# Hybrid encoder block: the output projection takes its PSUM banks one at a time, in another chunk order, and the order planner waits longer before transposes

## The chip, the cores and the metric

The kernel runs on one core of one Trainium2 chip. The metric is the device time of one execution, in microseconds (us). The profiled execution also has a span, from its first to its last instruction; about 2.2 us of the device time lie outside it.

## The reference, cut to what matters

The input is x, 1024 tokens of 1024 channels, float32. One layer, then a last RMSNorm:

```python
hn = rms_norm(h, ln_g)
proj = hn @ w_in + b_in                      # 1024 x 3584
glu_a, glu_b, z_conv, q, k, v, z_att = split(proj)   # 512 columns each
y_conv = conformer_conv(glu_a, glu_b, ...)   # GLU, depthwise conv of 31 taps, LayerNorm, swish, 512 x 512 product
y_att  = neighbourhood_attention(q, k, v, rpb)       # 8 heads of 64 on a 16 x 64 grid, window 8 x 16
y_conv = grouped_rms_norm(y_conv, ..., 8) * silu(z_conv)
y_att  = grouped_rms_norm(y_att, ..., 8) * silu(z_att)
h = h + concatenate([y_conv, y_att]) @ w_out         # 1024 x 1024
out = rms_norm(h, final_g)
```

## The kernel before, in words

Every float32 product is made of three matmuls: each operand is split into a high part in a rounded float32 format (ACT copies it) and a low part, the rest (DVE or POOL subtracts), and high x high, low x high and high x low are added up in one PSUM bank. PSUM has eight banks of 128x512 float32; the program names them by tags: two each of `pj`, `s` and `tr`, one each of `o` and `ln`.

**The order planner.** The instructions of PE, ACT, DVE, POOL and SP stay in the order in which the program emits them, and each engine works through its own queue in that order. The order comes out of a planner, `Clock` (from line 93). The work is written as some dozens of Python generators ("streams") with a rank. The planner has a time of its own, `now`, which a matmul moves on by its planned duration (`mm`, `tp`), and a planned end for each of ACT, DVE and POOL (`queue`). A stream that yields a time is not taken up before `now` has come to it; among the streams that are due, `weave` (line 113) takes the one of lowest rank. Nothing waits on the chip for a planned time: what is planned sets only the order in each queue. On the chip, semaphores hold an instruction back until its inputs and its buffer are there, and all that is behind it on its engine with it. `Ring` (line 74) hands out buffers and banks by the same planned time.

**Margins.** A stream that wants to put a matmul or a transpose on PE after work on another engine yields the planned end of this work plus a margin. `PEL` (0.3) stands at the four places of `pointwise` (lines 864, 887, 907 and 928), `PEA` (0.15) in `stats` (312), in `turns` (739, the transposes of the softmax), in `attention` (782 before the products with v, for each of two groups of a block, and 794 before the transposes of the result), and in `head_out` (817, before the transposes of a pair of heads).

**The stages.** After the normalisation come the input projections (`proj`), the convolution's taps on DVE (`taps`) and the attention, 32 blocks of scores, softmax, turns and products with v. Then `pointwise(t)`, once for each of eight tiles of 128 tokens: transposes into bank `tr` (tile ln), LayerNorm, transposes into bank `ln` (lnb), the 512 x 512 product in bank `ln` (pw), the grouped norm, and transposes back into bank `ln` (yt). A tile holds one of two buffers (xn) from its start to its yt, so that tile t+2 starts when tile t is through. The end of yt on ACT is noted in `ln_end[t]`.

**The last gates.** `final_gates` (from line 1074) makes the last two column blocks of z_conv for both halves of the tokens: four banks, `pj`, `pj`, `s`, `s`, 96 matmuls into tiles pz. `gated` (from line 953) then works off each bank: tanh on ACT into tile gz, two DVE instructions into z, which frees the bank, and a product on DVE that puts z into acc, the convolution's half of y. There is one gz buffer, so the four follow one another.

**The output projection.** The 1024 rows of w_out are eight chunks k of 128. Chunks 0 to 3 are of the convolution, 4 to 7 of the attention; `K_OUT` is 4, 5, 6, 7, 0, 1, 2, 3. `out_weights` splits the chunks into woh and wol (the low parts by turns on POOL and DVE). `split_y` splits y for each tile of tokens into yh and yl, from ya (attention) and acc (convolution); a tile 3 to 7 does so when buffers come free. `out_mm` (line 1152) emits the three matmuls of a tile, a chunk and a piece of columns (two pieces of 512 per tile; the last tile has 512, 256, 256). `finish` adds x, squares and sums on ACT, scales, and sends the tile out. `out_proj` (from line 1197) sets the order. It begins when all eight `ln_end` are there. Tiles 0, 1 and 2 go together: it first takes six banks (tr, tr, o, ln, pj, pj), and then goes chunk by chunk through all six. Tiles 3 to 7 come one by one, each piece with all its eight chunks. x_again loads x again for `finish`, two tiles ahead.

Of the kernel before, what the change touches and what calls it, by code (L numbers as in the profile page):

```python
# [21 lines left out]
NT = T // P  # L22
# [29 lines left out]
PQ = 0.2  # L52
KHY = (0, 1, 2)
BV = ("o", "ln")
PEL, PEA, PEB, MMO = 0.3, 0.15, 0.15, 0.0137
W_AHEAD = 12
TQ = 0.4
TURN = 0.02
# [8 lines left out]
def size(ap):  # L67
    n = 1
    for d in ap.shape[1:]:
        n *= d  # L70
    return n
# [88 lines left out]
def block(ctx: ExitStack, tc: tile.TileContext, x, xt, vecs, w_in, taps_w, pw_w, pw_b, tab0, tab1, tab2, w_out, final_g, out):  # L160
# [14 lines left out]
    ck = Clock(nc)  # L175
# [5 lines left out]
    RB, NB = {"pj": r_pj, "s": r_s, "tr": r_tr, "o": r_o, "ln": r_ln}, {"pj": 2, "s": 2, "tr": 2, "o": 1, "ln": 1}  # L181
    r_hn, r_hy = ring(0), ring(0)

    def U(name, dt=F32, shape=(P, 1024)):
        return big.tile(list(shape), dt, tag="u", name=name)

    def half_tile(tag, name, dt=F32, bufs=1):
        return att.tile([P, 512], dt, tag=tag, bufs=bufs, name=name)
# [4 lines left out]
    def bank(tag, name, bufs=2):  # L193
        return ps.tile([P, 512], F32, tag=tag, bufs=bufs, name=name)
# [460 lines left out]
    def group_scale(src, ms, sq, sums=None):  # L655

        g = sq.rearrange("p (g d) -> p g d", d=64)
        t = ck.act(out=g, in_=src, func=AF.Square, scale=0.125)
        yield t
        t = ck.dve("tensor_reduce", t, in_=g, out=ms, axis=mybir.AxisListType.X, op=ALU.add) + 0.5  # L660
        ck.q["dve"] = t
        if sums is None:
            t = ck.dve("tensor_scalar", out=ms, in0=ms, scalar1=EPS, scalar2=None, op0=ALU.add)
        else:
            ck.dve("scalar_tensor_tensor", out=sums, in0=sums, scalar=EPS, in1=sums, op0=ALU.mult, op1=ALU.mult)
            t = ck.dve("tensor_tensor", out=ms, in0=ms, in1=sums, op=ALU.add)
        yield t
        t = ck.gps("tensor_tensor", 1.65, t, out=ms, in0=ms, in1=mhalf, op=ALU.pow)
        return t


    def grid(ap):
        return ap.rearrange("p (r c) -> p r c", c=GW)
# [93 lines left out]
    def attention():  # L767
        for n, (i, a, b) in enumerate(blocks):
# [34 lines left out]
            if b < 3:  # L803
                r_o.put(t)
            else:
                ck.spawn(head_out(i, a, ytok, po), -1)

    def head_out(i, a, ytok, po):
        ms = sm.tile([P, 8], F32, tag="ms", name=f"ams{2 * i + a}")
        src = ytok[:, :, a, :]  # L810
        t = yield from group_scale(src, ms, po, sumss[2 * i + a])
        r_o.put(t - 1.6)
        t = ck.gps("tensor_tensor", 1.05, t, out=src, in0=src, in1=ms.unsqueeze(2).broadcast_to([P, 8, 64]), op=ALU.mult)
        if a == 0:
            return
        yield from r_u.get()
        yield t + PEA
        y = U(f"ya{i}")
        yg = grid(y)
        for b2 in range(2):  # L820
            yield from r_tr.get()
            pt = bank("tr", f"yat{i}_{b2}")
            for e in range(4):
                ck.tp(pt[:, e * P:(e + 1) * P], ytok[:, 4 * b2 + e].rearrange("p a d -> p (a d)"), ident)
            for b in range(2):
                c0 = 32 * b2 + 16 * b
                t = ck.act(out=yg[:, :, c0:c0 + 16],
                           in_=pt[:, 256 * b:256 * b + 256].rearrange("p (r c) -> p r c", c=16),
                           func=AF.Copy, scale=hcol(V_GNA + i))
            r_tr.put(t)  # L830
            yield
        r_y.put()
        ya[i] = y, t
# [208 lines left out]
    K_OUT = list(range(4, 8)) + list(range(4))  # L1042
# [109 lines left out]
    def out_mm(po, t, k, sl):  # L1152
        while (t, k) not in ysp or k not in woh:
            yield ck.now + 0.1
        yh, yl, a = ysp[t, k]
        yield max(a, woh[k][1])
        ck.mm(po, yh[:, k, :], woh[k][0][:, sl], k == K_OUT[0], False)
        ck.mm(po, yh[:, k, :], wol[k][:, sl], False, False)
        ck.mm(po, yl[:, k, :], woh[k][0][:, sl], False, k == K_OUT[-1])

    def pieces(t):

        ends = (0, 512, 768, 1024) if t == NT - 1 else (0, 512, 1024)
        return [slice(a, b) for a, b in zip(ends, ends[1:])]

    def finish(t, n, sl, po, ss):
        while t not in xr:
            yield ck.now + 0.1
        x_ = xr[t][:, sl]
        e = ck.dve("tensor_tensor", out=x_, in0=po, in1=x_, op=ALU.add)  # L1170
        yield e
        junk = half_tile(("uh", "ul")[n % 2], f"oj{t}_{n}", bufs=1 + n % 2)[:, :size(po)]
        e = ck.act(e, out=junk, in_=x_, func=AF.Square, scale=1.0 / 32.0, accum_out=ss[:, n:n + 1])
        ck.dve("tensor_tensor", out=x_, in0=x_, in1=fg[:, sl], op=ALU.mult)
        yield e
        if n == 0:
            ck.gps("tensor_scalar", 0.2, e, out=ss[:, 0:1], in0=ss[:, 0:1], scalar1=EPS, scalar2=None, op0=ALU.add)
            return
        e = ck.gps("tensor_tensor", 0.3, e, out=ss[:, 0:1], in0=ss[:, 0:1], in1=ss[:, n:n + 1], op=ALU.add)
        if sl.stop < D:  # L1180
            return
        rs = sm.tile([P, 1], F32, tag="rs", name=f"ors{t}")
        e = ck.gps("tensor_tensor", 0.47, e, out=rs, in0=ss[:, 0:1], in1=mhalf[:, :1], op=ALU.pow)
        yield e
        for m in range(2):
            x_ = xr[t][:, 512 * m:512 * m + 512]
            if m == 0:
                d = ck.dve("tensor_scalar", e, 0.55, out=x_, in0=x_, scalar1=rs, scalar2=None, op0=ALU.mult)
            else:
                d = ck.act(e, out=x_, in_=x_, func=AF.Copy, scale=rs)  # L1190
            yield d
            nc.sync.dma_start(out=out2[t * P:(t + 1) * P, 512 * m:512 * m + 512], in_=x_)
        r_u.put(d + 3.0)
        r_xr.put(d + 3.0)
        state["out"] = t

    def out_proj():
        tags = ("tr", "tr", "o", "ln", "pj", "pj", "s", "s")
        i = 0
        while len(ln_end) < NT:  # L1200
            yield ck.now + 0.2
        for ts in ((0, 1, 2), (3,), (4,), (5,), (6,), (7,)):
            po, ss = {}, {}
            for t in ts:
                ss[t] = sm.tile([P, 3], F32, tag="st", name=f"oss{t}")
                for n, sl in enumerate(pieces(t)):
                    tag = tags[i % 8]
                    i += 1
                    yield from RB[tag].get()
                    po[t, n] = bank(tag, f"out{t}_{n}", NB[tag])[:, :sl.stop - sl.start], tag  # L1210
            if len(ts) > 1:
                for k in K_OUT:
                    for t in ts:
                        for n, sl in enumerate(pieces(t)):
                            yield from out_mm(po[t, n][0], t, k, sl)
                for t in ts:
                    for n, sl in enumerate(pieces(t)):
                        ck.spawn(finish(t, n, sl, po[t, n][0], ss[t]), -1)
                        RB[po[t, n][1]].put(ck.now + 1.5)
            else:  # L1220
                t = ts[0]
                for n, sl in enumerate(pieces(t)):
                    for k in K_OUT:
                        yield from out_mm(po[t, n][0], t, k, sl)
                    ck.spawn(finish(t, n, sl, po[t, n][0], ss[t]), -1)
                    RB[po[t, n][1]].put(ck.now + 1.0)
                    yield
            for t in ts:
                for _ in range(2):
                    (r_hy if t % 4 < 3 else r_u).put()  # L1230

    fgs = []

# [14 lines left out]
    ck.spawn(out_tiles(), 0)  # L1248
    ck.spawn(x_again(), 0)
    ck.spawn(out_proj(), 6)  # L1250
    ck.weave(lambda: state["out"] == NT - 1 and len(ck.streams) == 0)
    in_order.__exit__(None, None, None)
# [47 lines left out]
```

## Time and profile before

| what | us |
|---|---|
| median of 3 runs | 570.06 (568.01 to 571.66) |
| the profiled execution | 567.91 |
| its span | 565.7 |
| PE busy | 529.6 (94%) |
| DVE busy | 430.3 (76%) |
| ACT busy | 274.1 (48%) |
| POOL busy | 172.0 (30%) |

The page gives busy time by engine, the span in 40 slices, the chain of work that ended last and the costliest groups. PE is TensorE, PEld its weight loads, DVE is VectorE, ACT is ScalarE, POOL is GpSimd, SP issues the DMAs. Matmuls overlap, and the ends of their rows are modelled: what counts is the distance from one start to the next. L130 and L136 are the helper lines of matmul and transpose, L141, L145 and L150 those of ACT, DVE and POOL, so that a row is told apart by its tiles (out<-woh,yh).

### The profile page before, as it was taken

How to read it: one execution, taken by the hardware profiler on the slowest of the kernel's cores; microseconds unless marked ns; L12 is line 12 of the kernel's file. 1: busy time of each engine (PE TensorE's matmuls, PEld its weight loads, DVE VectorE, ACT ScalarE, POOL GpSimd, SP SyncE). 2: the span in 40 equal slices, each digit the busy share in tenths (PEclk: the TensorE clock that was granted, in tenths of full speed). 3: DMA queues.
4: the chain of work that ended last, by engine and by line, in shares of the span. 5: the costliest groups of instructions: out<-in, count | busy, mean ns of one | idle time of the engine just before them, and what ended most of it. 6: DMA issues, size and time to landing. Idle time of an engine off the chain costs nothing. (4 is left out here: it accounts for less than half of the span.)

```text
span 565.7 us, 7506 instructions
## 1 busy us (share of the span) xinstructions
PE 529.6 (94%) x2656; PEld 438.2 (77%) x2656; DVE 430.3 (76%) x709; ACT 274.1 (48%) x656; POOL 172.0 (30%) x142
## 2 busy tenths in 40 slices
PE   5998999999999999989998999998999977999995
PEld 4886788898878888878876787786877765888884
DVE  4459999989999989999899988767645468056342
ACT  7765421265633555535563755848455462053221
POOL 4422232221043404060043545226254270022121
PEclk9999999999999999999999999999999996999999
DMA  8941115521225331453234341010006311004442
GB/s 303 405 154 49 37 37 147 133 85 42 84 64 143 94 96 46 105 130 103 76 95 121 77 132 64 22 38 5 34 0 261 112 35 41 0 1 148 162 136 75
DMA packets 22613, 55.04 MB, mean 97 GB/s; under 512 B 3120, under 2 KB 3248, under 8 KB 22576
## 3 DMA queue, kind: packets, MB, share of 16 engines
q1 hardware_dynamic: 22288, 54.47, 30.8%
q8 instruction: 21, 0.34, 0.3%
q14 instruction: 16, 0.13, 0.1%
q10 hardware_dynamic: 288, 0.09, 0.1%
HBM read 40.92 MB, written 4.19 MB: 80 GB/s over the span
## 5 line engine op out<-in xcount | busy, mean ns | idle before, releaser
L145 DVE SCALAR_TENSOR_TENSOR acc<-glu,dwc,acc 128x512 f32<-128x512 f32 (+25 forms) x150 | 172.9, 1182 | 0.7
L150 POOL TENSOR_TENSOR wl<-wr,wh 128x512 fp32r<-128x512 f32 x48 | 79.7, 1677 | 200.0 <-ACT wh L141 200.0
L130 PE MATMUL out<-woh,yh 128*128 128x512 f32 (+1 forms) x136 | 53.0, 390 | 7.1 <-DVE z L145 7.1
L130 PE MATMUL pz<-hi,wh 128*128 128x512 f32 x128 | 53.2, 415 | 1.1 <-DVE ya L145 1.1
L130 PE MATMUL out<-wol,yh 128*128 128x512 f32 (+1 forms) x136 | 52.5, 386 | 0.0
L130 PE MATMUL out<-woh,yl 128*128 128x512 f32 (+1 forms) x136 | 52.5, 386 | 0.0
L130 PE MATMUL pz<-hi,wl 128*128 128x512 f32 x128 | 50.2, 392 | 0.0
L130 PE MATMUL pz<-lo,wh 128*128 128x512 f32 x128 | 50.1, 392 | 0.0
L141 ACT ACTIVATE prob<-s,mx 128x264 f32<-128x264 f32 (+1 forms) x64 | 33.4, 528 | 27.2 <-DVE mx L145 27.1
L141 ACT ACTIVATE wh<-wr 128x512 fp32r<-128x512 f32 x56 | 32.5, 625 | 23.0 <-DMA wr<-in_w_in 7.7
L145 DVE TENSOR_TENSOR xr<-out,xr 128x512 f32<-128x512 f32 (+1 forms) x17 | 11.0, 658 | 39.8 <-PE out L130 31.0
L145 DVE TENSOR_TENSOR ptl<-ptp,pth 128x512 fp32r<-128x512 f32 x64 | 37.8, 614 | 0.0
L141 ACT ACTIVATE pth<-ptp 128x512 fp32r<-128x512 f32 x64 | 32.5, 547 | 9.5 <-PE ptp L136 8.4
L130 PEld LDWEIGHTS out<-woh,yh 128*128 128x128 f32 x136 | 26.4, 194 | 13.1 <-DVE z L145 8.3
L136 PE MATMUL ptp<-ident,prob 128*128 128x128 f32 x224 | 32.8, 273 | 1.5 <-DVE ptl L145 1.4
L130 PE MATMUL pb<-hi,wh 128*128 128x512 f32 x64 | 26.2, 410 | 7.4 <-ACT wh L141 5.5
L145 DVE CUSTOM_DVE_ANT_0 s<-s,bias 128x264 f32<-128x264 f32 (+1 forms) x64 | 30.2, 511 | 0.9 <-PE s L130 0.9
L130 PE MATMUL po<-pth,v 128*128 128x256 f32 x112 | 29.8, 291 | 0.6 <-DVE v L145 0.4
L130 PE MATMUL po<-ptl,v 128*128 128x256 f32 x112 | 29.3, 290 | 1.1 <-DVE ptl L145 1.1
L130 PEld LDWEIGHTS out<-wol,yh 128*128 128x128 f32 x136 | 26.5, 195 | 4.9
L130 PEld LDWEIGHTS out<-woh,yl 128*128 128x128 f32 x136 | 26.3, 194 | 5.0
L136 PEld LDWEIGHTS ptp<-ident,prob 128*128 128x128 f32 x224 | 25.9, 140 | 4.7 <-issue 2.0
(151 smaller groups left out, 1352.6 us busy)
## 6 DMA issues: line engine op xcount, KB each, us to landing
wr<-in_w_in SPq DMA_DIRECT2D x27, 512.0 KB, 3.7
bias<-in_tab SPq DMA_DIRECT2D x16, 276.0 KB, 2.8
xc<-in_xt SPq DMA_DIRECT2D x16, 256.0 KB, 5.4
acc<-in_x SPq DMA_DIRECT2D x8, 512.0 KB, 6.3
wor<-in_w_out SPq DMA_DIRECT2D x8, 512.0 KB, 5.0
xr<-in_x SPq DMA_DIRECT2D x8, 512.0 KB, 3.8
out<-xr SPq DMA_DIRECT2D x16, 256.0 KB, 2.3
kh<-kh SPq DMA_DIRECT2D x24, 128.0 KB, 2.4
```

The lines of the kernel that those rows point to most:

```text
L130: self.nc.tensor.matmul(out, lhsT=lhsT, rhs=rhs, start=start, stop=stop)
L136: self.nc.tensor.transpose(out=out, in_=in_, identity=identity)
L141: self.nc.scalar.activation(**k)
L145: getattr(self.nc.vector, fn)(**k)
L150: getattr(self.nc.gpsimd, fn)(**k)
```

## The change

Two constants become larger, one margin in `head_out` changes its name, and the loops of `out_proj` are written anew. A function `part(t, ks)` emits the matmuls of tile t and chunks ks, piece by piece, and takes a bank only when it comes to a piece that has none. It is called for tiles 0, 1, 2 with the four chunks of the attention, then for tiles 0, 1, 2 with the four of the convolution, then for tiles 3 to 7 with all eight. `finish` is started after a piece's last chunk. The order in which the tags are used and the start condition on `ln_end` stay.

```diff
-PEL, PEA, PEB, MMO = 0.3, 0.15, 0.15, 0.0137
+PEL, PEA, PEB, MMO = 0.8, 0.3, 0.15, 0.0137
...
@@ head_out
         yield from r_u.get()
-        yield t + PEA
+        yield t + PEL
         y = U(f"ya{i}")
...
@@ out_proj
-        for ts in ((0, 1, 2), (3,), (4,), (5,), (6,), (7,)):
-            po, ss = {}, {}
-            for t in ts:
+        po, ss = {}, {}
+
+        def part(t, ks):
+
+            if t not in ss:
                 ss[t] = sm.tile([P, 3], F32, tag="st", name=f"oss{t}")
-                for n, sl in enumerate(pieces(t)):
-                    tag = tags[i % 8]
-                    i += 1
-                    yield from RB[tag].get()
-                    po[t, n] = bank(tag, f"out{t}_{n}", NB[tag])[:, :sl.stop - sl.start], tag
-            if len(ts) > 1:
-                for k in K_OUT:
-                    for t in ts:
-                        for n, sl in enumerate(pieces(t)):
-                            yield from out_mm(po[t, n][0], t, k, sl)
-                for t in ts:
-                    for n, sl in enumerate(pieces(t)):
-                        ck.spawn(finish(t, n, sl, po[t, n][0], ss[t]), -1)
-                        RB[po[t, n][1]].put(ck.now + 1.5)
-            else:
-                t = ts[0]
-                for n, sl in enumerate(pieces(t)):
-                    for k in K_OUT:
-                        yield from out_mm(po[t, n][0], t, k, sl)
+            for n, sl in enumerate(pieces(t)):
+                if (t, n) not in po:
+                    yield from banks(t, n, sl)
+                for k in ks:
+                    yield from out_mm(po[t, n][0], t, k, sl)
+                if ks[-1] == K_OUT[-1]:
                     ck.spawn(finish(t, n, sl, po[t, n][0], ss[t]), -1)
                     RB[po[t, n][1]].put(ck.now + 1.0)
                     yield
-            for t in ts:
+            if ks[-1] == K_OUT[-1]:
                 for _ in range(2):
                     (r_hy if t % 4 < 3 else r_u).put()
+
+        def banks(t, n, sl):
+            nonlocal i
+            tag = tags[i % 8]
+            i += 1
+            yield from RB[tag].get()
+            po[t, n] = bank(tag, f"out{t}_{n}", NB[tag])[:, :sl.stop - sl.start], tag
+
+        for t in range(3):
+            yield from part(t, K_OUT[:4])
+        for t in range(3):
+            yield from part(t, K_OUT[4:])
+        for t in range(3, NT):
+            yield from part(t, K_OUT)
```

## Rows read from the trace of the kernel before

**Rows 1.** The windows: PE, PEld, DVE, ACT, POOL busy, granted clock, DMA share, GB/s.
```profile
50.00:350.00 300.00, 288.94 (x1512) 241.34 (x1510) 286.83 (x442) 142.23 (x349) 88.72 (x52) 1.00 0.33 92
```

**Rows 2.** The chain that ended last, in order of time: start, us, what.
```profile
456.61 3.92 PE pz L130 x17
...
472.22 86.93 PE out L130 x393
...
561.38 0.72 ACT xr L141
```

**Rows 3.** Waits of PE over the span: us in total, times, longest.
```profile
PE out L130 <- DVE z L145: 7.1, 2, 6.2
...
PE lnb L136 <- DVE xn L145: 3.3, 3, 1.1
...
PE yat L136 <- POOL ytok L150: 1.8, 2, 1.5
...
PE yt L136 <- POOL xn L150: 1.1, 2, 0.8
PE po L130 <- DVE ptl L145: 1.1, 5, 0.3
```

**Rows 4.** Windows of tile out: us, PE busy, PEld busy, DVE busy, granted clock, DMA.
```profile
460.58:463.50 2.92, 2.88 (x12) 2.07 (x11) 0.00 (x0) 1.00 0.01 3
463.50:469.63 6.13, 0.00 (x0) 0.00 (x1) 0.00 (x0) 0.84 0.24 86
469.63:477.51 7.88, 6.94 (x16) 4.98 (x16) 0.00 (x0) 0.50 0.21 67
477.51:500.51 23.00, 23.00 (x102) 19.03 (x101) 0.00 (x0) 0.99 0.00 1
500.51:552.00 51.49, 51.49 (x229) 42.66 (x228) 9.44 (x14) 1.00 0.36 123
```

**Rows 5.** Timeline of all engines between the last gates and the output projection.
```profile
449.01 0.42 DVE L145 TENSOR_TENSOR yl<-acc,yh 128x256 fp32r<-128x256 f32 x1
...
454.33 0.28 DVE L145 TENSOR_TENSOR yl<-ya,yh 128x128 fp32r<-128x128 f32 x1
...
459.23 1.21 DVE L145 TENSOR_TENSOR wol<-wor,woh 128x1024 fp32r<-128x1024 f32 x1
...
460.58 0.39 PE L130 MATMUL out<-woh,yh 128*128 128x512 f32 x1
...
462.65 5.80 DVE L145 TENSOR_TENSOR wol<-wor,woh 128x1024 fp32r<-128x1024 f32 x2 [2.21 <-issue]
...
468.82 0.75 DVE L145 SCALAR_TENSOR_TENSOR z<-pz,cols,gz 128x512 f32<-128x512 f32 x1
...
469.63 0.79 PE L130 MATMUL out<-woh,yh 128*128 128x512 f32 x1 [6.17 <-DVE z L145]
...
471.42 0.75 DVE L145 SCALAR_TENSOR_TENSOR z<-pz,cols,gz 128x512 f32<-128x512 f32 x1
...
472.22 0.80 PE L130 MATMUL out<-woh,yh 128*128 128x512 f32 x1 [0.94 <-DVE z L145]
...
477.09 1.43 DVE L145 TENSOR_TENSOR yl<-acc,yh 128x256 fp32r<-128x256 f32 x4
```

**Rows 6.** Timeline of PE: the transposes that end pointwise tiles 1, 3, 5 and 7.
```profile
351.87 0.66 PE L136 MATMUL yt<-ident,xn 128*128 128x128 f32 x4 [0.84 <-POOL xn L150]
...
385.20 0.60 PE L136 MATMUL yt<-ident,xn 128*128 128x128 f32 x4
...
425.55 0.60 PE L136 MATMUL yt<-ident,xn 128*128 128x128 f32 x4
...
456.01 0.60 PE L136 MATMUL yt<-ident,xn 128*128 128x128 f32 x4
```

**Rows 7.** Timeline of SP: the loads of x for the finish, two by two.
```profile
464.11 9.13 SPq L1150 DMA_DIRECT2D xr<-in_x  x2
...
512.73 2.34 SPq L1150 DMA_DIRECT2D xr<-in_x  x2
```

## Prediction

> **What bounds the kernel now.** I read the windows first. From 50 to 350 us PE is busy for 288.94 us of 300 and DVE for 286.83 [rows 1]: two engines close to full, and a reordering can win only what PE idles there, 11 us. Then the chain of work that ended last: behind 472.22 us it is one run of 393 output matmuls, 86.93 us, and a tail on DVE, ACT and SP [rows 2]. So the end of the kernel is set by when the output projection gets going, and by whether PE stays fed and at its full clock until then. Third, the waits of PE: the longest, 7.1 us in two pieces, is the output projection waiting for tile z [rows 3]. The windows of tile out show what stands there: 12 matmuls up to 463.50, nothing for 6.13 us, then a stretch of 7.88 us at a granted clock of 0.50, and only then full speed [rows 4].
>
> The timeline says why. The 12 matmuls are chunk 4 of the four pieces in banks tr, tr, o and ln. The fifth piece needs a bank pj, which the last gates hold until their first z, and this z comes late because two weight splits, 5.80 us, stand ahead of it on DVE [rows 5]. The sixth needs the second pj and waits for the second z. PE works in order, so chunks 5 to 7 of the first four pieces, which need no pj, stand behind this wait.
>
> **The change part by part.**
>
> *The new order.* It removes and adds no matmul: 408 output matmuls as before. Counting back from the chain's 393, 15 of them had started before 472.22, and 12 more by 477.51, one each 0.43 us. At full speed one takes 0.2255 us (102 in 23.00) [rows 4]; I use 0.227, to be safe against records that are missing. Between 460.58 and 477.51, 16.93 us, PE therefore did 27 x 0.227 = 6.1 us of work. What is lost is 10.8 us: 6.17 and 0.94 us of waits with some start-up around them, and 2.6 us by the half clock (12 matmuls at 0.441 instead of 0.227).
>
> How much of it comes back depends on when each piece of the new order is ready, with PE starting at 460.58:
>
> - Tiles 0 and 1, chunks 4 to 7: 48 matmuls, 10.9 us, until 471.5. Their yl from ya were done by 454.6, and the last of their weights, chunk 7's, at 459.23 + 1.21 = 460.44, while PE comes to it after nine matmuls, at 462.6. No wait.
> - Tile 2, chunks 4 to 7: needs the first pj at 471.5; its z ends at 468.82 + 0.75 = 469.57. It needs the second at 474.2; that z ends at 472.17. No wait.
> - Tile 0, chunks 0 to 3, from 476.9: the weights were done at 462.65 + 5.80 = 468.45, and the yl of chunks 0 and 1 by 449.43. Chunks 2 and 3 come after six matmuls, at 478.3. They need the last gates: four yl between 477.09 and 478.52, tile 0's first, at about 477.5 [rows 5].
>
> So in the rows as they stand all 10.8 us come back, with 0.7 us to spare at the last point. As the gates could come a little later in the new order, I charge 0.5 us there.
>
> *One bank after another.* Before, 102 matmuls that go round six banks took 0.2255 us each, and 229 that stay in one bank 0.2248 [rows 4], so 12 or 24 matmuls in one bank cost what 3 did: 102 x 0.0007 = 0.07 us, nothing. The Trainium skill (TensorE: Matmul & The Clock Gate, section "A second HAM failure mode: psum-queue depth-cycling") speaks of a kernel in which cycling through PSUM banks makes the clock swing between its two levels. By that rule the old stretch of six banks would have run partly at the half level, and the new order would win there beyond the sum; this trace disagrees, with 0.99 granted in it.
>
> *The finish.* Tiles 0 to 2 are finished one after another, 24 matmuls or 5.4 us apart, no longer all three at 501. Tile 0 gets its x from the loads issued at 464.11; tile 2's is loaded after tile 0 left and may land late, as the third was issued at 512.73 before [rows 7]. DVE then waits, not PE: the eight banks go round, and tile 4 is the first to want a used one, some 20 us after tile 0 freed it. I cost this at nothing; if that cover were gone, the price would be a few us in the middle. The tail behind the last matmul, 559.15 to 565.7, stays.
>
> *The margins.* They add no instruction and no wait on the chip. They put a transpose or a product later in PE's queue, behind other matmuls. Where PE now waits at such a point, the wait shrinks by at most the added margin: lnb, three waits of about 1.1, 0.5 each, 1.5 us; yt, one of 0.84 and a short one, 0.7; yat, with 0.65 more, 0.9 in two; po, five short ones, 0.15 each, 0.7 [rows 3]. At most 3.8 us. The other end is a loss. Tiles 1, 3, 5 and 7 of `pointwise` follow one another through one of the two buffers, from yt to yt [rows 6], with four margins each: 4 x 4 x 0.5 = 8.0 us if every one lay on the path. The last yt is at 456.01, and behind it PE still has 3.92 us of pz [rows 2], so the first 3.9 us cost nothing. A margin lengthens the path only where PE comes right at the due time. The trace has PE waiting at few of these 32 points, so at most others it arrives late anyway; I take a third of the 8.0, 2.7 us, which is inside the cover. For the gain I take 1.7 of the 3.8, since what is put in front can make a wait elsewhere.
>
> *Sum.* 567.91 - 10.8 + 0.5 - 1.7 = 555.9 us against the profiled execution. This one lies 2.15 us under the median of the runs shown, so the median of the new kernel should be 555.9 + 2.15 = 558.05, say 558.
>
> **The rivals.**
>
> *The pointwise chain becomes the wait.* If all 8.0 us go on the path, the last yt comes at 464.0 and PE runs out of pz: 8.0 - 3.9 = 4.1 us idle, and, as after the 6.13 us before, some 2.6 us at half clock. The start condition on `ln_end` makes this possible, since no output matmul is queued ahead of that yt. For it speaks the unbroken sequence of yt rows; against it the 3.9 us of cover. 567.91 - 10.8 + 4.1 + 2.6 = 563.8, in the median 566: same.
>
> *The wait only moves.* The four gates follow one another at 2.60 us (468.82 to 471.42) [rows 5]. If they come one such period later, the yl are late by 2.6 - 0.7 = 1.9 us at tile 0's chunk 2, and with the half clock behind it 2.6 more. Without the 0.5 of the sum, 555.4 + 4.5 = 559.9, in the median 562: still faster. If the order of chunks did not decouple the projection from pj at all, because a stream ahead of it in the planner put the waiting matmul first, the kernel would stay at about 568 to 570; the code gives no way for that, as a bank is asked for only in its own piece.
>
> *Slower: the attention pays for its margins.* A block has four places with `PEA`, one in `turns` and three in `attention`, 0.15 us each: 0.6 us x 32 blocks = 19.2 us if the blocks were a serial chain. Then 567.91 - 10.8 + 19.2 = 576.3, in the median 578. It decides from 10.8 / 32 = 0.34 us per block on. For it speaks that PE does wait for results of the attention (po, five times) [rows 3]; against it that PE has other work in nearly all of this time, 288.94 of 300 [rows 1], so a later block lets a projection go first, and the work stays the same.
>
> **How the numbers follow.** Forecast 0.70; the pointwise chain 0.12; the wait that moves 0.10; the attention 0.06; no effect at all 0.02. A measurement of this kernel tells about 1% (5.7 us) from no change. Faster by over 1%, below 564.4: the forecast nearly whole and the wait that moves, 0.79. Within 1%: the pointwise chain, no effect, part of the edges, 0.15. Slower: the attention 0.06. The range: at the lower end 567.91 - 10.8 - 3.8 + 2.15 = 555.5 with all gain of the margins, and 4.5 us less for waits that a new order loses by luck (PE idles 11 us from 50 to 350), 551. At the upper end the pointwise chain, 566.
>
> **What would show it.** In the new profile PE should have no wait for z of over 1 us, the granted clock should stay at 1.00 where it now reads 0.50 [rows 4], and the last output matmul should end some 11 us or more earlier than at 559.15, with the tail behind it as long as before. A bubble just before yt of tile 7 would show the pointwise chain; one at a yl of acc, six matmuls into tile 0's second part, the moved wait; more PE idle between 50 and 350, the attention. I am wrong if the output projection starts much later than at 460 us, or if a gap with a half clock stands anywhere near it.

## The result and the profile after

The new kernel takes 551.25 us in the median of four runs (550.33 to 554.22), the kernel before 569.5; the ratio is 0.9686 with a 95% interval of 0.9637 to 0.9735. That is 18 us less, where the prediction had 12. The profiled execution of the new kernel took 554.22 us, the most of its four runs, and that of the kernel before 567.91 us, less than any of its four (568.01 to 571.66): the two traces differ by 13.7 us, and 4.6 us of the difference between the medians are not in them.

First the output projection. The windows of tile out in the changed kernel, to be held against [rows 4] (us, PE busy, PEld busy, DVE busy, granted clock, DMA):

```profile
458.06:477.50 19.44, 19.44 (x86) 16.13 (x86) 0.20 (x1) 1.00 0.16 54
477.50:500.50 23.00, 23.00 (x103) 19.02 (x103) 4.44 (x7) 1.00 0.38 134
500.50:538.00 37.50, 37.50 (x167) 31.07 (x166) 5.01 (x8) 1.00 0.25 87
```

From its first matmul at 458.06 PE is busy all the time, at the full clock (1.00); the 6.13 us of nothing and the 7.88 us at 0.50, the lower of the clock's two levels (1.2 instead of 2.4 GHz), are gone. The timeline of the same stretch, against [rows 5]:

```profile
453.51 0.60 PE L136 MATMUL yt<-ident,xn 128*128 128x128 f32 x4
...
457.83 0.39 PE L130 MATMUL pz<-hi,wl 128*128 128x512 f32 x1
458.06 0.39 PE L130 MATMUL out<-woh,yh 128*128 128x512 f32 x1
...
460.13 5.87 DVE L145 TENSOR_TENSOR wol<-wor,woh 128x1024 fp32r<-128x1024 f32 x2 [2.19 <-issue]
...
466.37 0.75 DVE L145 SCALAR_TENSOR_TENSOR z<-pz,cols,gz 128x512 f32<-128x512 f32 x1
...
474.46 1.42 DVE L145 TENSOR_TENSOR yl<-acc,yh 128x256 fp32r<-128x256 f32 x4
```

DVE does what it did, two slow weight splits and then the gates: from the start of the splits to the four yl it takes 14.3 us (460.13 to 474.46), 14.4 before (462.65 to 477.09). PE comes to the first pj at 458.06 + 10.9 = 469.0, 1.8 us after its z, and to chunk 2 of tile 0 at 475.7, 0.9 us after the first of the four yl (474.46 + 0.36). The order fits with little to spare, as worked out.

Then the waits of PE before the output projection, 20 to 450 us (total, times, longest), against [rows 3]:

```profile
PE s L130 <- DMA kh<-kh: 2.6, 1, 2.6
PE pb L130 <- DVE sg L145: 1.9, 1, 1.9
PE lnb L136 <- DVE xn L145: 1.7, 2, 0.9
PE po L130 <- DVE ytok L145: 1.6, 2, 1.1
PE po L130 <- DVE ptl L145: 1.3, 5, 0.5
...
PE yat L136 <- POOL ytok L150: 0.4, 1, 0.4
PE yt L136 <- POOL xn L150: 0.4, 1, 0.4
```

Some old waits shrank or went, and two stand here that were not there or hardly: 2.6 us for a copy of kh and 1.6 us for ytok. So the list was not just shortened, it was drawn anew. The sum of all its lines fell from 16.3 to 11.6 us. The two traces also show the cause: ahead of the output projection PE has the same 2248 matmuls and transposes in both, but in another sequence of tiles.

### The profile page after: what moved, and what is told of

Its sections match the earlier page's. It is cut to its first block, busy times and chain, and to the rows that moved or that the text cites. A ratio compares the mean times of both kernels' runs of the same rounds, so it can differ in the third digit from the quotient of the medians.

```text
span 552.1 us, 7499 instructions
## 1 busy us (share of the span) xinstructions
PE 527.0 (95%) x2656; PEld 439.8 (80%) x2656; DVE 425.6 (77%) x709; ACT 273.9 (50%) x656; POOL 169.4 (31%) x142
## 5 line engine op out<-in xcount | busy, mean ns | idle before, releaser
L145 DVE SCALAR_TENSOR_TENSOR acc<-glu,dwc,acc 128x512 f32<-128x512 f32 (+25 forms) x150 | 170.5, 1168 | 0.7
L150 POOL TENSOR_TENSOR wl<-wr,wh 128x512 fp32r<-128x512 f32 x48 | 76.1, 1603 | 180.4 <-ACT wh L141 180.4
L130 PE MATMUL out<-wol,yh 128*128 128x512 f32 (+1 forms) x136 | 51.2, 377 | 0.0
L130 PE MATMUL out<-woh,yl 128*128 128x512 f32 (+1 forms) x136 | 51.2, 376 | 0.0
L130 PE MATMUL out<-woh,yh 128*128 128x512 f32 (+1 forms) x136 | 51.2, 376 | 0.0
L141 ACT ACTIVATE prob<-s,mx 128x264 f32<-128x264 f32 (+1 forms) x64 | 33.6, 531 | 14.4 <-DVE mx L145 14.3
L141 ACT ACTIVATE oj<-xr 128x512 f32<-128x512 f32 (+1 forms) x17 | 10.3, 607 | 42.1 <-DVE xr L145 40.9
L141 ACT ACTIVATE os<-po 128x256 f32<-128x256 f32 x32 | 12.3, 386 | 36.3 <-PE po L130 36.2
```

The lines of the kernel that those rows point to most:

```text
L130: self.nc.tensor.matmul(out, lhsT=lhsT, rhs=rhs, start=start, stop=stop)
L141: self.nc.scalar.activation(**k)
L145: getattr(self.nc.vector, fn)(**k)
L150: getattr(self.nc.gpsimd, fn)(**k)
```

## Experiments

All ratios are against the kernel before, with their 95% intervals; a per cent is 5.7 us, and differences in us are taken from the ratios. Each edit is shown against the kernel named in its text.

**The new loops alone**: the changed kernel with the old margins.

```diff
-PEL, PEA, PEB, MMO = 0.8, 0.3, 0.15, 0.0137
+PEL, PEA, PEB, MMO = 0.3, 0.15, 0.15, 0.0137
...
-        yield t + PEL
+        yield t + PEA
```

> The new loops of out_proj with the old margins (0.3, 0.15, and PEA in head_out). My theory: the order of the chunks alone gives back the wait for the two pj banks and the half clock behind it, 10.8 to 11.0 us, so about 558.6 us against 569.5, ratio 0.981; PE without a gap from the first to the last output matmul, granted clock 1.00 there. Rival: the order carries the whole change, 18 us, and the margins nothing: 551 us, ratio 0.968.

Measured: 558.55 us, ratio 0.9792 (0.9766 to 0.9818), 11.9 us less. In its trace PE is busy for all of the 87.4 us from the first output matmul to the last, at a granted clock of 1.00. The rival falls.

**The margins alone**: the kernel before with the new constants and `PEL` in `head_out`.

```diff
-PEL, PEA, PEB, MMO = 0.3, 0.15, 0.15, 0.0137
+PEL, PEA, PEB, MMO = 0.8, 0.3, 0.15, 0.0137
...
-        yield t + PEA
+        yield t + PEL
```

> The wider margins alone, out_proj as before. My theory: they win what the two profiles show ahead of the first output matmul, 2 to 2.5 us: about 567 us, ratio 0.996; the wait for z and the half clock stay. Rival: they carry what is left of the change's 18 us after the order's 11: 7 us, 562.5 us, ratio 0.988. Second rival: they win nothing by themselves, 569.5 us.

Measured: 563.66 us, ratio 0.9892 (0.9860 to 0.9923), 6.2 us less. Here the rival holds: the margins carry what the order leaves. Within the intervals the two parts simply multiply: 0.9792 x 0.9892 = 0.9686, the ratio of the whole change. The traces bear it out: ahead of the output projection PE's sequence of tiles is that of the kernel before in the new loops alone, and that of the changed kernel in the margins alone.

**Order or banks?** Two kernels with the old margins part the two things that the new loops do; their edits are shown against the new loops alone. The first has the new order, but takes all six banks in front:

```diff
+        for t in range(3):
+            for n, sl in enumerate(pieces(t)):
+                yield from banks(t, n, sl)
         for t in range(3):
             yield from part(t, K_OUT[:4])
```

> The new order of chunks, old margins, but all six banks of tiles 0 to 2 taken in front, as before. My theory: only the order in PE's queue counts, and a bank taken earlier in the planner moves nothing on the chip, so the same time as with the new loops and old margins, about 558.6 us, within 1 us of it. Rival: taking the banks one by one is what frees PE: then some 7 to 11 us slower than that run, near the kernel before.

Measured: 557.34 us, 0.9777 (0.9750 to 0.9804), the same as the new loops within the intervals. The second takes the banks one by one in the old order:

```diff
-        for t in range(3):
-            yield from part(t, K_OUT[:4])
-        for t in range(3):
-            yield from part(t, K_OUT[4:])
+        for k in K_OUT:
+            for t in range(3):
+                yield from part(t, [k])
```

> The counterpart of taking the banks in front: the banks taken one by one, but in the old order, chunk by chunk through the six pieces; old margins. My theory: PE's queue is the same as before, so the fifth piece's chunk 4 waits for pj as before and the time is that of the kernel before, ratio 1.00, 570 us. Rival: taking the banks one by one brings part of the order's 2.1% by itself: 0.985 to 0.99.

Measured: 570.49 us, 1.0004 (0.9985 to 1.0023). Its waits of PE begin with the old one:

```profile
PE out L130 <- DVE z L145: 6.9, 2, 6.2
```

So the gain is all in the order of the matmuls in PE's queue. When the planner takes a bank moves nothing on the chip that these runs can tell.

**The clock behind the wait.** The kernel before, with work that does nothing ahead of the output projection:

```diff
             if len(ts) > 1:
+                while (0, 4) not in ysp or 4 not in woh:
+                    yield ck.now + 0.1
+                for _ in range(27):
+                    nc.tensor.matmul(po[0, 0][0], lhsT=ysp[0, 4][0][:, 4, :], rhs=woh[4][0][:, 0:512], start=True, stop=True)
                 for k in K_OUT:
```

> The kernel before, with 27 additional matmuls of 512 columns (about 6.1 us) into the first output bank ahead of its first real matmul, which overwrites them. They fill the wait for the first pj bank with work that does nothing. My theory: the half clock costs 2.6 us by itself; the fillers keep the clock up and the wait is as long as they are, so the kernel becomes about 2.6 us faster although it does more: 566.9 us, ratio 0.995; granted clock 1.00 behind the wait. Rival: the slow stretch behind the wait is not the clock's answer to the idle time; then the fillers win nothing, 569.5 us or up to 1 us more.

Measured: 565.74 us, 0.9925 (0.9898 to 0.9952): 6 us more of work, and 4.3 us faster, with an interval of 2.7 to 5.8. The chain of its trace, against the 86.93 us of [rows 2], and its window of tile out where the kernel before had a granted clock of 0.50 [rows 4]:

```profile
473.27 84.25 PE out L130 x393
```

```profile
470.00:478.00 8.00, 6.26 (x27) 4.56 (x26) 0.00 (x0) 1.00 0.19 66
```

The same 393 matmuls take 2.68 us less, with the clock up. That the slow stretch is the clock's answer to the idle time is shown, and the trace gives it the size that the sum had. What the ratio gives beyond that lies in the spread of the kernel before (last section).

**Which margin?** The new loops with one margin each, shown against the changed kernel:

```diff
-PEL, PEA, PEB, MMO = 0.8, 0.3, 0.15, 0.0137
+PEL, PEA, PEB, MMO = 0.8, 0.15, 0.15, 0.0137
...
-        yield t + PEL
+        yield t + PEA
```

> The new loops of out_proj, of the margins only PEL at 0.8 (pointwise); PEA stays at 0.15 and head_out at PEA. The new loops with the old margins were 2.1% faster than the kernel before, with all margins 3.1%. My theory: pointwise is where PE waited longest (lnb 3.3, ln 1.8, yt 1.1 us before, 1.7, 0 and 0.4 after), so PEL carries two thirds of the 1.1% (6 us): ratio about 0.972, 554.5 us. Rival: the attention's 128 places carry them, then 0.979, 558.5 us.

Measured: 560.42 us, 0.9829 (0.9800 to 0.9859). `PEL` alone wins nothing over the new loops (0.9792).

```diff
-PEL, PEA, PEB, MMO = 0.8, 0.3, 0.15, 0.0137
+PEL, PEA, PEB, MMO = 0.3, 0.3, 0.15, 0.0137
...
-        yield t + PEL
+        yield t + PEA
```

> The new loops of out_proj, of the margins only PEA at 0.30 (stats, turns, attention, head_out); PEL stays at 0.3. My theory: PEA carries one third of the margins' 1.1%: ratio about 0.976, 556.5 us, and the new wait of PE for the copies of kh (2.6 us in the changed kernel) comes with it. Rival of the prediction: the attention loses by its margins; then slower than the new loops alone, over 0.979. Second rival: it carries all of it, 0.969, 552.5 us.

Measured: 552.96 us, 0.9699 (0.9679 to 0.9719). `PEA` wins it all, and the wait for kh did not come with it. My shares, two thirds and one third, were wrong. The windows say where half of it lies: 200 to 300 us in the new loops alone, then with `PEA` 0.30 (PE, PEld, DVE, ACT, POOL busy, clock, DMA):

```profile
200.00:300.00 100.00, 96.96 (x543) 82.14 (x543) 95.25 (x167) 52.19 (x137) 23.22 (x15) 1.00 0.31 92
```

```profile
200.00:300.00 100.00, 99.79 (x572) 85.17 (x571) 97.18 (x175) 53.52 (x142) 23.87 (x15) 1.00 0.33 97
```

PE is busy 2.8 us longer there, of the 5.3 us between the two kernels, and starts 29 matmuls and transposes more, in the middle of the attention. But is it the size of the margin?

**Margin or order?** Two more sizes of `PEA`, with `PEL` 0.3, shown against the last kernel:

```diff
-PEL, PEA, PEB, MMO = 0.3, 0.3, 0.15, 0.0137
+PEL, PEA, PEB, MMO = 0.3, 0.22, 0.15, 0.0137
```

> The new loops of out_proj, PEL 0.3, PEA 0.22 (between 0.15, ratio 0.979, and 0.30, ratio 0.970). Theory of the margin: the time falls steadily with PEA, as each step takes something off each wait: 0.974 to 0.975, 555.5 us. Theory of the order: any change of a margin gives another order of the whole queue, and its waits are drawn anew; then the time lies anywhere between 0.967 and 0.985 with no trend, and follows the sum of PE's waits in its own trace.

```diff
-PEL, PEA, PEB, MMO = 0.3, 0.3, 0.15, 0.0137
+PEL, PEA, PEB, MMO = 0.3, 0.4, 0.15, 0.0137
```

> As the last, PEA 0.40. Theory of the margin: at or a little below 0.970, since little is left to win: 0.967 to 0.971. Theory of the order: anywhere between 0.967 and 0.985.

And the changed kernel with a smaller `PEL`:

```diff
-PEL, PEA, PEB, MMO = 0.8, 0.3, 0.15, 0.0137
+PEL, PEA, PEB, MMO = 0.5, 0.3, 0.15, 0.0137
```

> The changed kernel with PEL 0.5 in place of 0.8, PEA 0.30. Theory of the margin (PEL hardly matters next to PEA): between the kernel with PEL 0.3 and the changed one, 0.969 to 0.970, 552 us. Theory of the order: anywhere between 0.967 and 0.985.

Measured: 552.89 us, 0.9696 (0.9672 to 0.9719), for 0.22; 558.21 us, 0.9787 (0.9766 to 0.9809), for 0.40; 551.19 us, 0.9664 (0.9644 to 0.9684), with `PEL` 0.5. Over `PEA` 0.15, 0.22, 0.30, 0.40 the ratio goes 0.979, 0.970, 0.970, 0.979: no steady fall, and 0.40 gives all of it back. The theory of the margin misses all three, the last one narrowly. That of the order allowed so much (0.967 to 0.985) that it hardly could miss, and four sizes do not exclude a valley with its bottom near 0.2 to 0.3. What speaks for the order is that nothing on the chip waits for a margin, so that it can act through the queues alone, and that single waits come and go from one size to the next. The times go largely with the sum of PE's waits in each trace, 20 to 450 us, here for all kernels with the new order of chunks:

| kernel (PEL, PEA) | sum of PE's waits, us | ratio |
|---|---|---|
| 0.5, 0.30 | 9.8 | 0.9664 |
| 0.8, 0.30 (the change) | 11.6 | 0.9686 |
| 0.3, 0.22 | 11.7 | 0.9696 |
| 0.3, 0.30 | 13.1 | 0.9699 |
| 0.3, 0.40 | 14.9 | 0.9787 |
| 0.3, 0.15 | 15.8 | 0.9792 |
| 0.3, 0.15, banks in front | 16.4 | 0.9777 |
| 0.8, 0.30, late copies (below) | 17.2 | 0.9828 |
| 0.8, 0.15 | 17.2 | 0.9829 |
| 1.3, 0.45 (below) | 19.1 | 1.0224 |

From the first row to the last but one the waits grow by 7.4 us and the time by 1.65%, 9.4 us. Neighbours can't be told apart: the banks in front have 0.6 us more of waits than the new loops, and the same queue. The last row stands off: its long waits lie behind 450 us. The kernel with `PEL` 0.5 is the quickest of the study; its interval overlaps that of the change, so it is as fast as the change, and faster than the kernel before.

**One wait taken away by hand.** The changed kernel waits 2.6 us for a copy of kh, which the planner thinks lands after 2.8 us.

```diff
@@ k_out, both places
-        yield ck.now + 2.8
+        yield ck.now + 4.2
```

> The changed kernel, with the planner told that the copies of kh and kl land 4.2 us after their issue instead of 2.8. My theory: the scores of the last pair no longer stand in PE's queue ahead of their keys; the wait of 2.6 us and the stretch at a granted clock of 0.89 behind it go: 3 us faster than the changed kernel, ratio about 0.963, 548.5 us. Rival: the scores come later and the attention's end with them, and what is won goes to another wait: 0.969, as the changed kernel.

Measured: 560.13 us, 0.9828 (0.9805 to 0.9850), 8 us slower than the changed kernel. The wait for kh is gone, and a longer one stands in its place:

```profile
PE lnb L136 <- DVE xn L145: 5.6, 2, 5.2
```

Here the last yt starts at 463.69 and the first output matmul right behind it, at 464.10, without any pz between them.

**Wider still.**

```diff
-PEL, PEA, PEB, MMO = 0.8, 0.3, 0.15, 0.0137
+PEL, PEA, PEB, MMO = 1.3, 0.45, 0.15, 0.0137
```

> The changed kernel with still wider margins, PEL 1.3 and PEA 0.45. Theory of the margin: a little faster or the same, 0.965 to 0.969, unless the chain of pointwise tiles comes late: with 4 x 4 x 1.0 = 16 us against the old margin, of which a third (5.3 us) on the path and 3.9 us covered, it would begin to cost 1.4 us. Theory of the order: anywhere between 0.967 and 0.985.

Measured: 583.52 us, 1.0224 (1.0199 to 1.0249): slower than the kernel before, by 13 us, with the good order of chunks in it, and outside what either theory allowed. The timeline of PE shows the rival of the prediction, the pointwise chain:

```profile
467.07 0.39 PE L130 MATMUL pz<-hi,wl 128*128 128x512 f32 x1
469.47 0.65 PE L130 MATMUL pw<-pwh,uh 128*128 128x512 f32 x1 [2.02 <-ACT uh L141]
...
473.28 0.80 PE L130 MATMUL pw<-pwh,ul 128*128 128x512 f32 x1 [2.73 <-DVE ul L145]
...
486.31 1.12 PE L136 MATMUL yt<-ident,xn 128*128 128x128 f32 x4 [8.99 <-POOL xn L150]
487.08 0.78 PE L130 MATMUL out<-woh,yh 128*128 128x512 f32 x1
```

The last pz starts at 467.07, and tile 7 still has its product and its yt to come. PE waits 2.0, 2.7 and 9.0 us for it, with a granted clock of 0.65 from 467 to 487 us, and the first output matmul stands right behind that yt. In the changed kernel 4.2 us of pz followed the last yt; here they have all gone before it. These three waits are 13.7 of the 29.0 us by which the output projection starts later than in the changed kernel (487.08 instead of 458.06); 7.5 us more are waits from 20 to 450 us. Whether the chain is late by the margins on its own path or by the new order ahead of it is not shown: both constants were changed at once.

## Why the prediction was right, and where a term was off

The forecast of 558 us and the 551.25 us measured lie 6.8 us apart, and the measured time is 0.25 us above the lower end of the stated range. That the range reached so far down is due to the 4.5 us put there for waits that a new order loses by luck; the gain worked out with all of the margins ended at 555.5. The order of chunks was foreseen by its mechanism, the size of the whole was not.

*What bounds the kernel.* Right. The wait for pj and the clock behind it were the largest single loss.

*The new order.* 10.8 us worked out; 11.9 measured (10.4 to 13.3). In the traces, the way from the first to the last output matmul, start to start, fell from 98.3 us (460.6 to 558.9) to 87.2 (458.1 to 545.3), 11.0 us. The split into wait and clock holds too: 2.6 us worked out for the clock, 2.68 in the trace with fillers. The 0.5 us charged for a late gate was not needed.

*Banks.* That 12 or 24 matmuls in one bank cost what 3 do stands: 103 in 23.00 us, as 102 before. The rule on cycling through banks (the Trainium skill, TensorE: Matmul & The Clock Gate, section "A second HAM failure mode: psum-queue depth-cycling") has nothing to explain here: the granted clock reads 0.99 in the old stretch and 1.00 in the new one.

*The finish* cost nothing: DVE waited once for x, 3.1 us, and PE not at all. The last output matmul starts 6.8 us ahead of the end in both traces.

*The margins* are the term that was mis-sized: 1.7 us taken, at most 3.8 thought possible, 6.2 measured (4.4 to 8.0). The step that failed is "Where PE now waits at such a point, the wait shrinks by at most the added margin". It keeps the queue's order and shortens each wait in place. The runs show instead that a changed margin reorders the queue. In the two traces the waits on the prediction's list shrank by 3.5 us together, inside its bound, but those that it left out fell by 5.2 us and rose by 4.0. One of them in the kernel before, 20 to 450 us:

```profile
PE ln L136 <- DVE ptl L145: 1.8, 1, 1.8
```

It went whole, although `PEB`, the margin of banks, was not touched, and it is no matter of `PEL` in front of these transposes: with `PEL` alone at 0.8 it still stands at 1.8 us. What rose is kh, from nothing to 2.6 us, and ytok, from 0.2 to 1.6. The bound of 3.8 was therefore none for the whole queue, and the word "margin" misled: its size has no steady price.

*The rivals.* The pointwise chain did not decide at these margins: the last yt came at 453.51, 2.5 us sooner than before. The third that I took of the full path was not tested at these margins. At `PEL` 1.3 with `PEA` 0.45 the chain is late, and PE's waits for it are 13.7 us, far more than the 1.4 us that the same reckoning gave there. That the attention would pay for its margins is refuted at 0.30: it gained.

## What to carry to other kernels

On an engine that works in order, put the work that needs a late buffer behind all the work that doesn't; the bound is found by listing, piece by piece, when PE comes to it and when it is ready. A constant of a planner need have no price per unit: it draws a new order, so bound its effect by all waits that the engine has, in both directions, and choose it by trying several and timing each; the sum of the waits in each trace says where the time went. Before widening delays in a chain that runs beside the engine's other work, see how much of that work is left when the chain ends: here it was 4 us, and in the kernel that had none left the engine waited for the chain.

## What the runs showed that I had not expected

The same queue does not always reach the same point at the same time. Up to the output projection the kernel with the banks in front and the one that takes them one by one in the old order have the queue of the kernel before; PE's sequence of tiles is the same in all three traces. Their windows from 50 to 100 us (PE, PEld, DVE, ACT, POOL busy, granted clock, DMA), in this sequence:

```profile
50.00:100.00 50.00, 46.81 (x203) 37.70 (x202) 49.62 (x54) 15.58 (x27) 12.54 (x7) 1.00 0.25 77
```

```profile
50.00:100.00 50.00, 47.26 (x198) 37.87 (x197) 48.64 (x54) 16.96 (x29) 12.66 (x8) 0.97 0.22 69
```

Both have a wait of 1.9 us for sg in it. In one the clock stays up, in the other it falls for a while, and the second begins the output projection at 463.9 instead of 460.6. The profiled execution of the kernel before is of the first kind and that of the changed kernel of the second, which goes the way of the 4.6 us that the two traces don't show. The trace of the new loops alone is of the second kind too (0.97 from 50 to 100 us). Held against it, the changed kernel starts the output projection 5.5 us earlier (458.06 instead of 463.55): that is what the margins gave, like against like, beside 6.2 us by the ratio.

The same holds for the fillers. Of the eleven runs of the kernel before beside them, four have a mean granted clock of 0.988 or 0.989, as its profiled execution (0.989), and took 568.7 us in the mean; seven have 0.985 or 0.986 and took 570.9. The profiled execution with fillers is of the first kind, and its four runs, at 0.996 to 0.998, took 565.75 in the mean: 3.0 us less than the first group, where the trace gave 2.68.

A second one is the size of a small step: 1.4 us in one assumed time of landing moved the whole kernel by 8 us.
